# Two half blocks first, casts by DMA, and a GpSimd queue that carries the loads: a fused matmul, gelu, matmul on one core

## The chip, the cores and the metric

The kernel runs on one core of one Trainium2 chip. The metric is the device time of one execution in microseconds (us); the median of several runs is compared. One profiled execution gives the trace. TensorE is the matmul engine, VectorE and ScalarE do element-wise work, GpSimd does some of it too and issues DMAs of its own, and SyncE only issues DMAs.

## The reference

```python
# x: [16, 512, 768] f32, w1: [768, 3072], b1: [3072], w2: [3072, 768]
y = np.matmul(x, w1) + b1
y = 0.5 * y * (1.0 + erf(y / np.sqrt(2.0)))     # gelu
return np.matmul(y, w2).astype(np.float32)
```

The 16 x 512 leading entries are one axis of 8192 rows.

## The kernel before

All matmuls take fp16 operands and add in fp32. To spare TensorE work, both large matmuls use a Strassen-like scheme: 20 products of operand sums take the place of 24 plain products. `P1_WOPS` and `P1_XOPS` list the sums of W1 tiles and of x tiles, `P1_ORD` the 20 products in their order, and `P1_OPS` how partial results in PSUM are copied (C), added (A) and finished (F). `P2_...` are the same for the second matmul.

**First matmul and gelu.** Rows 0 to 511 are done without the scheme, in *plain units*: `plain_unit(u)` for u = 0 to 5, four output tiles each, 6 matmuls of 128x512 per tile (L608). The other rows go in *blocks* of three row groups. `BLK` has six: a half block (256 rows per group), four full blocks (512 rows per group), and a half block. A block has six units (three pairs in a half block). A unit has 60 matmuls of 512 columns (a pair of half units 120 of 256 columns, L739). Each full unit or pair also takes 12 additions with a PSUM operand on VectorE (L318 and L316, into `vt`), 4 copies out of PSUM (L323, ScalarE mostly) and 12 gelu tiles of 512 columns (L444, ScalarE; two instructions of 256 in a half block). `finish` writes gelu to one of `NGST` = 8 buffers, and a store on SyncE's queue (L449, `gd<-ar`) takes it to DRAM. A buffer is free again when its store has landed.

**W1.** `w1_load` brings 24 f32 pieces through SyncE (L374), VectorE or ScalarE casts each (L325, L323), and `w1_ops` makes the 20 operand tiles of each of the six units, 384 columns wide, on VectorE or GpSimd. All six plain units come ahead of the first half block.

**x.** `load_x(b)` casts the rows of a block to fp16 in DRAM by GpSimd DMAs of 256 rows (L593, `xd<-in_x_dram`: 3 for a half block, 6 for a full one) and brings them transposed into SBUF by DMA transposes on SyncE's queue (L595, `ar<-xd`). `x_sums(b)` then makes 13 operand sums per block, on VectorE (one instruction) or GpSimd (three).

**W2.** `w2_build(j)`, eight times, loads a piece of W2 by a GpSimd DMA, makes 12 sums and 2 negated copies on GpSimd, and stores 16 tiles to the DRAM buffer `w2d` by 16 SyncE DMAs (L718).

**Second matmul.** 16 units of 512 rows, 160 matmuls of 128x384 each (L841), 2560 in all. It reads W2's 16 tiles from `w2d` (L785) into the room of W1, and gelu from `gd` (L806), makes 16 sums per unit on VectorE (128x1024), and stores to `out` (L864). The loads are issued by SyncE.

**Order.** All instructions are written out by a planner (`Sched`) when the kernel is built. It keeps a modelled time for each engine and for DMA, and starts the task that can begin first; urgent and background tasks differ by a due time. Its costs (`dve_tt`, `act_ps`, `pool_tt`, the DMA rates) thus decide only the order on each engine. On the chip each engine runs its list in order and waits for the data of each instruction. `add(..., after=, order=)` sets constraints for the planner; only the data that instructions share becomes a wait on the chip.

Of the kernel before, what the change touches and what calls it, by code (L numbers as in the profile page):

```python
# [13 lines left out]
P = 128  # L14
# [9 lines left out]
P1_ORD = [(0, 0, 0), (3, 1, 1), (1, 2, 2), (2, 3, 3), (4, 4, 4), (3, 5, 5), (2, 6, 6), (4, 7, 7), (3, 8, 8), (1, 9, 9), (5, 10, 10), (4, 11, 11), (1, 12, 12), (3, 13, 13), (2, 14, 14), (4, 15, 15), (3, 16, 12), (2, 17, 16), (1, 18, 17), (4, 19, 14)]  # L24
# [5 lines left out]
P1_OPS = [('C', [(1, 0, 2, 0)], -1), ('C', [(1, 0, 3, 0)], -1), ('C', [(1, 0, 3, 2)], -1), ('C', [(1, 0, 4, 0)], -1), ('A', [(-1, 1, 1, 0), (1, 0, 3, 1)], -1), ('A', [(1, 1, 4, 0), (-1, 0, 3, 4)], -1), ('F', [(1, 1, 5, 0)], 0), ('F', [(-1, 0, 2, 3)], 1), ('A', [(-1, 1, 1, 0), (1, 0, 2, 2)], -1), ('F', [(1, 1, 8, 0)], 2), ('A', [(-1, 1, 3, 0), (1, 0, 1, 2)], -1), ('F', [(1, 1, 10, 0)], 3), ('F', [(1, 0, 1, 3)], 4), ('A', [(-1, 1, 3, 0), (1, 0, 4, 1)], -1), ('A', [(1, 1, 13, 0), (-1, 0, 4, 4)], -1), ('F', [(1, 1, 14, 0)], 5), ('F', [(-1, 0, 3, 3)], 6), ('A', [(-1, 1, 2, 0), (-1, 0, 4, 2)], -1), ('F', [(1, 1, 17, 0)], 7), ('F', [(1, 0, 4, 3)], 8), ('A', [(1, 1, 3, 0), (-1, 0, 1, 1)], -1), ('A', [(1, 1, 20, 0), (1, 0, 5, 0)], -1), ('F', [(1, 1, 21, 0)], 9), ('A', [(-1, 0, 1, 0), (1, 1, 0, 0)], -1), ('F', [(1, 1, 23, 0)], 10), ('A', [(1, 0, 0, 0), (1, 1, 1, 0)], -1), ('A', [(1, 1, 25, 0), (-1, 0, 2, 1)], -1), ('F', [(1, 1, 26, 0)], 11)]  # L30
# [54 lines left out]
class Task:  # L85
    __slots__ = ("eng", "fn", "nd", "outs", "reads", "alloc", "frees", "due", "key", "end",
                 "deps", "nbytes", "bulk", "lag", "gen", "started")


class Sched:  # L90


    def __init__(self):
        self.t = {e: 0.0 for e in ("PE", "DVE", "ACT", "POOL", "SP")}
        self.pe = []
        self.pp = 0
        self.avail = {e: [] for e in ("DVE", "ACT", "POOL", "SP")}
        self.dma = [0.0, 0.0, 0.0]
        self.key = 0
        self.left = 0  # L100
        self.pe_ideal = 10.0

    def add(self, eng, fn, reads=(), alloc=None, makes=None, after=(), frees=None, due=None, nbytes=0, bulk=0, order=(), lag=LAT):
# [4 lines left out]
        t.lag = lag  # L108
        t.end = None
# [34 lines left out]
    def _start(self, t, e):  # L144
        r = self.t[e]
        for d in t.deps:
            x = d.end + (0.0 if e in d.eng and len(d.eng) == 1 and e != "SP" else t.lag)
            if x > r:
                r = x
# [7 lines left out]
    def run(self, until=None):  # L157
        drift = 0.0
        while self.left:
# [47 lines left out]
            t.started = r  # L207
            if t.nbytes:
                self.t[e] = r + d
                self.dma[t.bulk] = max(self.dma[t.bulk], r + d) + t.nbytes / (320e3, 250e3, 200e3)[t.bulk]  # L210
# [23 lines left out]
def kernel(  # L234
# [27 lines left out]
    NGST = 8  # L262
    O_BLD = O_GST + NGST * 1024
    NBLD = 10
    O_END = O_BLD + 4608 + NBLD * 768
    NV = 8
# [6 lines left out]
    ident = main.tile([P, P], FP16, name="ident")  # L273
    ps = pps.tile([P, 8, 512], FP32, name="ps")
    gd = [drp.tile([P, HC, 512], FP16, name=f"gd{i}") for i in range(NU)]
    xd = drp.tile([R, K], FP16, name="xd")
    w2d = drp.tile([len(P2_WOUT), P, 8 * NB], FP16, name="w2d")
# [25 lines left out]
    def dve_ps(n):  # L303
        return (n / 0.96 + 215) / 1000

    def act_ps(n):
        return (n / 1.2 + 190) / 1000

    def pool_tt(n):
        return (n * 2.2 + 60) / 1000  # L310
# [24 lines left out]
    def w1_ap(u, w):  # L335
        return a16(O_W1 + (u * 20 + w) * W1T, 384)

    w1op = {}
    w1v = [[Val() for _ in range(20)] for _ in range(6)]
# [5 lines left out]
    WRING = Pool([O_XB + 3072 * i for i in range(6)])  # L345
    SRING = Pool([O_XA + 9216] + [O_SUM + (7 + 2 * i) * 3072 for i in range(4)])
    SRING.put(-1.0, O_BLD + 6144)
# [16 lines left out]
    wch = {}  # L364
    w1cast = []
    w1first = []

    def w1_load(u):
        sv = Val(SRING)
        parts = [Val() for _ in range(4)]  # L370
        for q in range(4):
            f = Val(WRING)
            c0 = (q * 6 + u) * P
            w1first.append(S.add({"SP": 0.45}, lambda e, f=f, c0=c0: nc.sync.dma_start(  # L374
                out=a32(f.slot, 768).rearrange("p (k c) -> p k c", c=P),
                in_=w1.rearrange("(kc p) c -> p kc c", p=P)[:, :, c0:c0 + P]),
                alloc=f, nbytes=P * 768 * 4))
            w1cast.append(S.add({"DVE": 0.50, "ACT": 0.75}, lambda e, f=f, q=q, sv=sv: scale_copy(
                e, a16(sv.slot + q * 1536, 768), a32(f.slot, 768), 1),
                reads=[f], alloc=sv if q == 0 else None, makes=[sv, parts[q]],  # L380
                after=[sv.prods[0]] if q else ()))
        wch[u] = (sv, parts)

    def w1_ops(u, due, after):
        sv, parts = wch[u]
        val = {}
        res = w1op[u] = []
        for i in range(8):
            val[i] = (parts[i // 2], lambda i=i, sv=sv: a16(sv.slot + i * 768, 384))
        outs = {}  # L390
        for w, (i, sg) in enumerate(P1_WOUT):
            outs.setdefault((i, sg), w)
        done = set()
        for (d, op, a, b) in P1_WOPS:
            w = outs.get((d, 1))
            assert w is not None
            va, fa = val[a]
            vb, fb = val[b]
            v = w1v[u][w]
# [503 lines left out]
```

## Time and profile before

| | us |
|---|---|
| median of 8 runs | 963.05 |
| lowest and highest | 961.81, 965.29 |
| profiled execution | 963.69 |
| its span, first to last instruction | 961.9 |
| TensorE busy | 873.5 (91%) |
| VectorE busy | 652.8 (68%) |
| ScalarE busy | 424.8 (44%) |
| GpSimd busy | 255.1 (27%) |

In lines of the profile, PE is TensorE, PEld its weight load, DVE VectorE, ACT ScalarE, POOL GpSimd, and SPq SyncE's DMA issues. L739 is line 739 of the kernel. "out<-in" names the tile or tensor written and read: `ar` is the large SBUF buffer, `ps` PSUM, `vt` partial results, `xd`, `w2d` and `gd` DRAM buffers. In the timeline a row gives start, duration, engine, line and operation, and in brackets how long the engine was idle before and what ended that.

### The profile page before, as it was taken

To read this page: it belongs to the slowest core of one execution; us is meant where nothing else is said; L and a number is where in the kernel's file an instruction comes from. 1 tells how busy PE (TensorE), PEld (TensorE's weight loads), DVE (VectorE), ACT (ScalarE), POOL (GpSimd) and SP (SyncE) were. 2 spreads that over 40 slices of the span, in tenths; PEclk is the share of its full clock that TensorE was granted. 3 is DMA by queue.
4 is the path that set the end of the run, shared out by engine and by line. 5 is a ranking of instruction groups with operands and counts; after the bars stand their busy time and mean duration, and the time that the engine had idled before them with its cause. 6 is when DMAs were issued, how large, how long until landed. Compare 5 with 4: busy or idle time off the path is not lost.

```text
span 961.9 us, 14602 instructions
## 1 busy us (share of the span) xinstructions
PE 873.5 (91%) x4924; PEld 484.9 (50%) x4924; DVE 652.8 (68%) x1009; ACT 424.8 (44%) x773; POOL 255.1 (27%) x270
## 2 busy tenths in 40 slices
PE   6688689788969879979998899999999999999997
PEld 2246534333424334434467566666666666666664
DVE  5989476368637746855677369777777777777763
ACT  5457466566746657757777412111111221211211
POOL 5777656158625600830430000000000000000000
PEclk9899799899979999999999999999999999999999
DMA  9989769887998557454669986555555555566611
GB/s 269 280 198 208 177 184 220 211 234 198 225 200 247 158 168 195 151 131 130 172 215 320 388 330 197 184 170 171 187 182 176 167 189 166 186 197 197 197 66 67
DMA packets 180332, 190.14 MB, mean 198 GB/s; under 512 B 57712, under 2 KB 171120, under 8 KB 173680
## 3 DMA queue, kind: packets, MB, share of 16 engines
q1 hardware_dynamic: 172320, 172.67, 58.0%
q0 software_dynamic: 4848, 16.52, 10.0%
q8 instruction: 38, 0.62, 0.3%
q10 hardware_dynamic: 3088, 0.01, 0.2%
q14 instruction: 38, 0.31, 0.1%
HBM read 106.97 MB, written 98.70 MB: 214 GB/s over the span
## 4 chain that ended last, share of the span: by engine, by line
PE 69%; DMA 11%; DVE 11%; issue 3%; ACT 3%; POOL 2%; DVEq 0%; SPq 0%; ACTq 0%; POOLq 0%
PE ps L841 43%; PE ps L739 23%; DMA gd<-ar 8%; DVE ar L318 6%; DVE vt L318 4%; ACT ar L444 3%; PE ps L608 2%; POOL ar L318 2%; DMA ar<-xd 1%; DMA b1t<-in_b_dram 1%; DVE ar L316 1%; DVE ar L325 1%; ACT vt L323 1%; DMA ar<-in_w_dram 1%; DMA w2d<-ar 0%
## 5 line engine op out<-in xcount | busy, mean ns | idle before, releaser
L739 PE MATMUL ps<-ar 128*128 128x512 f16 (+1 forms) x2160 | 412.6, 353 | 63.3 <-ACT vt L323 27.6
L841 PE MATMUL ps<-ar 128*128 128x384 f16 x2560 | 418.0, 327 | 2.7 <-ACT vt L323 2.7
L739 PEld LDWEIGHTS <-ar 128*128 128x128 f16 x2160 | 215.0, 100 | 260.9 <-issue 79.2
L841 PEld LDWEIGHTS <-ar 128*128 128x128 f16 x2560 | 251.0, 98 | 169.4 <-issue 4.8
L318 DVE TENSOR_TENSOR ar<-ar 128x1024 f16<-128x1024 f16 (+3 forms) x350 | 262.0, 766 | 16.4 <-DMA ar<-xd 9.0
L318 POOL TENSOR_TENSOR ar<-ar 128x384 f16<-128x384 f16 (+2 forms) x206 | 208.8, 1043 | 220.8 <-DMA ar<-xd 101.7
L318 DVE TENSOR_TENSOR vt<-vt,ps 128x512 f32<-128x512 f32 (+1 forms) x260 | 167.5, 644 | 128.5 <-PE ps L739 52.6
L323 ACT ACTIVATE vt<-ps 128x512 f32<-128x512 f32 (+1 forms) x232 | 123.4, 543 | 253.8 <-PE ps L841 229.1
L318 DVE TENSOR_TENSOR vt<-ps,vt 128x512 f32<-128x512 f32 (+1 forms) x230 | 147.6, 642 | 119.0 <-ACT vt L323 52.5
L444 ACT ACTIVATE ar<-vt,b1t 128x512 f16<-128x512 f32 (+1 forms) x288 | 176.3, 645 | 115.6 <-DVE vt L318 81.8
L444 ACT ACTIVATE ar<-ps,b1t 128x512 f16<-128x512 f32 (+1 forms) x168 | 98.8, 614 | 46.0 <-DMA gd<-ar 24.9
L323 ACT ACTIVATE ar<-vt 128x384 f32<-128x384 f32 x48 | 25.1, 523 | 108.2 <-DVE vt L318 87.0
L608 PE MATMUL ps<-ar 128*128 128x512 f16 x144 | 38.0, 424 | 11.0 <-DVE ar L325 11.0
L316 DVE SCALAR_TENSOR_TENSOR vt<-vt,ps 128x512 f32<-128x512 f32 (+1 forms) x46 | 29.3, 637 | 4.2 <-PE ps L841 1.5
L608 PEld LDWEIGHTS <-ar 128*128 128x128 f16 x144 | 14.7, 107 | 33.2 <-DVE ar L325 14.8
L318 DVE TENSOR_TENSOR ar<-vt 128x384 f32<-128x384 f32 x48 | 26.8, 557 | 1.6
L327 POOL TENSOR_SCALAR ar<-ar 128x384 f16<-128x384 f16 x20 | 23.9, 1204 | 13.8 <-DVE ar L325 10.7
L325 DVE CAST ar<-ar 128x768 f16<-128x768 f32 (+1 forms) x24 | 17.6, 742 | 9.3 <-DMA ar<-in_x_dram 5.9
L316 DVE SCALAR_TENSOR_TENSOR ar<-vt,ps 128x384 f32<-128x384 f32 x16 | 8.9, 555 | 21.9 <-PE ps L841 21.7
L323 ACT ACTIVATE ar<-ar 128x384 f16<-128x384 f16 (+2 forms) x31 | 15.9, 556 | 7.5 <-DVE ar L325 3.7
L593 POOL DMA_DIRECT2D xd<-in_x_dram x27 | 13.4, 503 | 0.0
L422 PE MATMUL ps<-ident,ar 128*128 128x128 f16 x60 | 5.9, 255 | 6.5 <-DVE ar L325 5.3
(17 smaller groups left out, 43.5 us busy)
## 6 DMA issues: line engine op xcount, KB each, us to landing
gd<-ar SPq DMA_DIRECT2D x384, 128.0 KB, 2.2
ar<-gd SPq DMA_DIRECT2D x48, 1024.0 KB, 5.6
out_dram<-ar SPq DMA_DIRECT2D x128, 192.0 KB, 5.6
w2d<-ar SPq DMA_DIRECT2D x128, 96.0 KB, 1.8
ar<-w2d SPq DMA_DIRECT2D x16, 768.0 KB, 7.5
xd<-in_x_dram POOLq DMA_DIRECT2D x27, 384.0 KB, 8.5
ar<-in_w_dram SPq DMA_DIRECT2D x24, 384.0 KB, 5.8
ar<-in_w_dram POOLq DMA_DIRECT2D x8, 576.0 KB, 8.6
```

The source lines that it names most:

```text
L316: eng.scalar_tensor_tensor(out=o, in0=a, scalar=-1.0, in1=b, op0=ALU.mult, op1=ALU.subtract)
L318: eng.tensor_tensor(out=o, in0=a, in1=b, op=ALU.add if op == "+" else ALU.subtract)
L323: nc.scalar.activation(out=o, in_=a, func=ACTF.Copy, scale=float(sg))
L325: eng.tensor_copy(out=o, in_=a)
L327: eng.tensor_scalar(out=o, in0=a, scalar1=-1.0, scalar2=None, op0=ALU.mult)
L422: nc.tensor.transpose(out=o[:, kc * P:(kc + 1) * P], in_=nat_ap(kc), identity=ident[:])
L444: ft.append(S.add({"ACT": act_ps(n)}, lambda e, y=y: nc.scalar.activation(out=a16(O_GST + g.slot * 1024 + y * n * 2, n), in_=src[1]()[:, y ...
L593: S.add({"POOL": 1.0}, lambda e, a=a, z=z: nc.gpsimd.dma_start(out=xd[a:z, :], in_=xf[a:z, :]), alloc=c, nbytes=256 * K * 4, bulk=1, after ...
L608: nc.tensor.matmul(out=ps[:, bv.slot, :], lhsT=a16(sv.slot + q * 1536 + kc * 256, P), rhs=a16(O_XT0 + kc * 1024, 512), start=(kc == 0), st ...
L739: nc.tensor.matmul(out=ps[:, bk, y * n:(y + 1) * n], lhsT=w1_ap(u + y, w)[:, kt * P:(kt + 1) * P], rhs=xa[:, kt * n:(kt + 1) * n], start=( ...
L841: nc.tensor.matmul(out=ps[:, bk, 0:NB], lhsT=xa[:, j, :], rhs=a16(w2v[w][1] + j * NB * 2, NB), start=(first and j == 0), stop=(j == 7), sk ...
```

## The change

**Order of the first part.** Plain units and the first half block alternate: plain units 0 and 1, the first pair of the half block, plain units 2 and 3, the second pair, and so on. The last half block moves to second place; the four full blocks follow.

**W1.** The staging now holds pairs of units. Only the first pair comes as f32 through SyncE and is cast by an engine (8 pieces). The other two come by 8 GpSimd DMAs that cast to fp16 on the way. `w1_ops` works on 768 columns, on VectorE alone (plain copies also on ScalarE).

**x.** `x_cast` issues the casts. Those of the second half block stand right behind W1's second pair in GpSimd's queue, those of the first full block right behind W1's third pair. For later blocks the first cast waits for the first x sum of the block two before, by a one-element GpSimd copy that reads that sum (`gated`). The transposes are planned behind given gelu stores of the block before (`mark`). All x sums are on VectorE.

**W2.** The 16 stores of a piece become two GpSimd DMAs (12 tiles made, 6 raw tiles). W2's 16 tiles and the gelu of the first two units of the second matmul are loaded by GpSimd; ten of the tiles and the first unit's loads are paced by one-element reads of gelu buffers of the last block.

**Room and planner.** `NGST` goes from 8 to 7, `NV` from 8 to 7. The planner gets other cost figures and treats the access of VectorE sums and GpSimd operations to SBUF as exclusive (`lock`). The order of units in the second matmul differs: 12, 13 and 14 are last.

GpSimd's list changes from 206 sums, 22 copies and 36 DMAs to 96 sums, 16 negated copies, 17 one-element copies and 84 DMAs. TensorE's instruction count stays.

```diff
-    NGST = 8
+    NGST = 7
-    NV = 8
+    NV = 7
...
+    def gated(gate, fn):
+        for v, ap in gate:
+            o = scr if ap.dtype == FP32 else scr16
+            nc.gpsimd.tensor_copy(out=o[0:1, 0:1], in_=ap[0:1, 0:1])
+        fn()
...
+    def w1_load(p):
...
+                else:
+                    hold = w1first[-1:] if p == 2 or q else x1l[-1:]
+                    w1first.append(S.add({"POOL": 0.85}, lambda e, c0=c0, o=o: nc.gpsimd.dma_start(
+                        out=a16(o, 1536).rearrange("p (k c) -> p k c", c=2 * P), in_=w1r[:, :, c0:c0 + 2 * P]),
+                        makes=[sv, wparts[2 * p][q], wparts[2 * p + 1][q]], nbytes=P * 1536 * 4,
+                        order=hold + sv.prods[:1], **first))
...
-    BLK = [((512, 768, 1024), 256)] + [((r, r + 512, r + 1024), 512) for r in range(1536, 7680, 1536)]
-    BLK.append(((1280, 7680, 7936), 256))
+    BLK = [((512, 768, 1024), 256), ((1280, 7680, 7936), 256)]
+    BLK += [((r, r + 512, r + 1024), 512) for r in range(1536, 7680, 1536)]
...
+    def x_cast(b):
...
+            gate = [blk_sum[b - 2]] if b > 2 and k == 0 else []
+            castq.append(S.add({"POOL": 1.0}, lambda e, a=a, z=z, gate=gate: gated(
+                [(g, a16(g.slot, 768)) for g in gate],
+                lambda: nc.gpsimd.dma_start(out=xd[a:z, :], in_=xf[a:z, :])),
+                alloc=c, reads=gate, nbytes=256 * K * 4, bulk=b > 2, order=w1first[-1:] + castq[-1:],
+                after=castq[-1:] if b > 2 else []))
...
+    w1_load(1)
+    x_cast(1)
+    w1_load(2)
+    x_cast(2)
...
+            m0, dm = {1: (22, 4), 2: (2, 3)}.get(b, (8, 5))
+            mark = blk_stores[b - 1][m0 + dm * k:m0 + dm * k + 1]
...
-            prev = [S.add({"DVE": dve_tt(3 * n), "POOL": 3 * pool_tt(n)}, fn, reads=[va, vb], alloc=v,
-                          order=prev, due=due)]
+            prev = [S.add({"DVE": dve_tt(3 * n)}, lambda e, fa=fa, fb=fb, v=v, op=op: comb(
+                e, a16(v.slot, 3 * n), op, fa(), fb()), reads=[va, vb], alloc=v, order=prev, due=due, lock=True)]
...
-            S.add({"SP": 0.45}, lambda e, fa=fa, w=w: nc.sync.dma_start(
-                out=w2d[w, :, j * NB:(j + 1) * NB], in_=fa()), reads=[va], makes=[w2sv[w]], nbytes=P * 768, bulk=1, lag=4.0)
+        S.add({"POOL": 1.0}, lambda e: nc.gpsimd.dma_start(
+            out=w2d[0:NOUT, :, j * NB:(j + 1) * NB].rearrange("w p n -> p w n"),
+            in_=a16(O_BO, NOUT * 384).rearrange("p (w n) -> p w n", n=NB)),
+            reads=made, frees=[ov], makes=[w2sv], nbytes=P * 768 * NOUT, bulk=1, lag=1.0, due=due)
...
             if b == 0:
-                for y in range(npair):
-                    w1_ops(u + y, S.pe_ideal - 1.0, {4: tr_nat, 5: x0cast}.get(u + y, ()))
+                plain_unit(u)
+                plain_unit(u + 1)
+                if u == 0:
+                    x1_transposes()
+                    xo = x_sums(b, S.pe_ideal, dur)
+                w1_ops(u // 2, S.pe_ideal - 1.0, ([], w1cast, tr_nat + x0cast)[u // 2])
...
-        S.add({"SP": 0.45}, lambda e, w=w, off=off: nc.sync.dma_start(out=a16(off, 8 * NB), in_=w2d[w]),
-              reads=[w2sv[w]], makes=[v], after=after, nbytes=P * W2T)
+        gate = [blk_g[len(BLK) - 1][(25 if w < 5 else 24) + 4 * w]] if w < 10 else []
+        w2l.append(S.add({"POOL": 1.0}, lambda e, w=w, off=off, gate=gate: gated(
+            [(g, a16(O_GST + g.slot * 1024, 512)) for g in gate],
+            lambda: nc.gpsimd.dma_start(out=a16(off, 8 * NB), in_=w2d[dslot[w]])),
+            reads=[w2sv] + gate, makes=[v], after=after, order=w2l[-1:], nbytes=P * W2T))
```

## The prediction

> **What bounds the kernel now.** I read four views in this order: the chain that ended last, the busy time by stage, the timeline of one stall, and the DMA queues. The chain comes first because it says which engine's time is on the path at all.
>
> ```profile
> PE 69%; DMA 11%; DVE 11%; issue 3%; ACT 3%; POOL 2%; DVEq 0%; SPq 0%; ACTq 0%; POOLq 0%
> PE ps L841 43%; PE ps L739 23%; DMA gd<-ar 8%; DVE ar L318 6%; DVE vt L318 4%; ACT ar L444 3%; PE ps L608 2%; POOL ar L318 2%; DMA ar<-xd 1%; DMA b1t<-in_b_dram 1%; DVE ar L316 1%; DVE ar L325 1%; ACT vt L323 1%; DMA ar<-in_w_dram 1%; DMA w2d<-ar 0%
> ```
>
> TensorE carries 69% of the path. The largest foreign piece is `gd<-ar`, the store of gelu results to DRAM. To place the losses I cut the span where the work changes: plain units, first half block, four full blocks, last half block, second matmul.
>
> ```profile
> 0.00:61.00 61.00, 43.04 (x204) 19.05 (x205) 47.13 (x75) 33.89 (x56) 41.58 (x49) 0.94 0.99 259
> 61.00:122.00 61.00, 44.30 (x349) 35.61 (x349) 45.01 (x60) 34.74 (x82) 42.53 (x41) 0.89 0.87 194
> 122.00:204.00 82.00, 68.18 (x291) 29.46 (x290) 45.30 (x66) 46.66 (x79) 40.52 (x47) 0.92 0.87 211
> 204.00:297.00 93.00, 80.75 (x357) 35.32 (x355) 58.81 (x83) 59.27 (x96) 55.48 (x57) 0.94 0.85 215
> 297.00:391.00 94.00, 84.59 (x381) 37.09 (x380) 61.73 (x87) 62.55 (x101) 27.96 (x27) 0.98 0.68 185
> 391.00:487.00 96.00, 89.96 (x408) 40.12 (x407) 63.47 (x90) 66.59 (x108) 42.94 (x48) 0.98 0.48 137
> 487.00:541.70 54.70, 47.46 (x399) 38.91 (x398) 37.85 (x59) 41.94 (x96) 4.06 (x6) 1.00 0.90 314
> 541.70:961.90 420.20, 415.24 (x2544) 249.36 (x2543) 293.49 (x496) 79.16 (x159) 0.00 (x0) 1.00 0.57 184
> ```
>
> Columns: length, then busy time of TensorE, its weight loads, VectorE, ScalarE and GpSimd, the granted clock, DMA share, GB/s. The second matmul is dense: 415 of 420 us. The first 541.7 us are not, and the clock falls to 0.89 to 0.94 where TensorE stops and starts. The timeline shows a typical stop:
>
> ```profile
> 157.69 2.96 POOL L593 DMA_DIRECT2D xd<-in_x_dram  x6
> 161.71 13.35 SPq L449 DMA_DIRECT2D gd<-ar  x6
> 170.53 0.72 ACT L444 ACTIVATE ar<-vt,b1t 128x512 f16<-128x512 f32 x1 [3.71 <-DMA gd<-ar]
> 173.79 0.69 ACT L444 ACTIVATE ar<-ps,b1t 128x512 f16<-128x512 f32 x1 [2.54 <-DMA gd<-ar]
> 174.53 19.72 PE L739 MATMUL ps<-ar 128*128 128x512 f16 x78 [6.02 <-ACT ar L444]
> ```
>
> Six casts of x are issued in 3 us. Then six gelu stores take 13.35 us, the eight gelu buffers fill, gelu waits for a landed store, and TensorE waits for the PSUM bank that gelu should have freed. The same follows the casts at 256, 330 and 417 us. The queues price it:
>
> ```profile
> q0 software_dynamic: 4848, 16.52, 10.0%
> xd<-in_x_dram POOLq DMA_DIRECT2D x27, 384.0 KB, 8.5
> ```
>
> The GpSimd queue (q0) wrote 16.52 MB in 10.0% of 961.9 us on all 16 engines: 96.2 us, 172 GB/s. A cast (0.393 MB) is 2.3 us of every DMA engine, six are 13.7 us.
>
> **Part 1, start and first half block (122 us now).** All engines' work for it, at unhindered rows. TensorE: the first 36 plain matmuls took 10.72 us; the other 108 at 5.34 us for 24 make 24.0; 36 transposes at 0.83 for 12 make 2.5; 360 half-width matmuls at 5.40 for 48 make 40.5. That is 77.7, from 10.96: 88.7. VectorE after the change: 39 W1 sums and 26 x sums, now 768 wide. A lone 384-wide one takes 0.35 us and a 1024-wide 0.687, between them 0.55: 35.9 us. Six negated sums (0.55 at 384; estimate 0.95 at 768) 5.7; 36 PSUM sums at 0.687 24.7; casts and evictions 9: together 75 from 4.3, so 80. ScalarE: 24 gelus at 0.675, 72 half ones at 0.455, 12 PSUM copies at 0.592, 14 W1 casts and copies at 0.84, the rest 9: 77 from 1.2, so 78. No engine alone needs more than 89.
>
> Before loses 33 us against 88.7. Of these 16.3 are TensorE waiting for VectorE's casts (11.0 and 5.3 in the waits). They go: 16 of 24 W1 casts are done by the GpSimd queue's transfers, and plain units alternate with Strassen-like units, so W1 is wanted in three portions. Another 10.2 (`ar<-xd` in the chain) was SyncE standing in transposes behind casts, with gelu stores queued behind it; the transposes now have fixed places later among the stores. In its place comes a new cost: 20 transfers of 0.393 MB (3 of x, 8 of W1, 9 casts) queue on GpSimd from about 18 us: 7.86 MB at 172 GB/s, 45.8 us of all engines. In the stall above a store passed each 2.2 us, or 0.45 per us; from 18 to 64 us that is 21 stores and 7 buffers, against some 33 gelus due: 5 late, 11 us. With a few us of W1 chains I keep about 15 of the 33: **104 us**, bounds 94 and 120.
>
> **Part 2, the second half block right behind.** 360 matmuls 40.5 us; ScalarE 72 at 0.455 and 9 copies 38. It was last and took 54.7, because W2 and gelu loads ran into its stores (9.2 and 9.4 us of `gd<-ar` in the chain there). Its x comes by three casts that are third in the GpSimd queue: 3.9 MB, 23 us alone, 50 when stores share, so by 68; needed near 104. **44 us**, bounds 41 and 50.
>
> **Part 3, four full blocks (365 us now).** Dense stretches (440 to 480 us) hold 94 matmuls in 20.00 us: 0.2128 each, 360 make 76.6, four 306.4; so 59 us are stall and slow clock. VectorE takes over all x sums: per block 72 at 0.685 and 13 at 0.95 (uncontended 1536-wide row) 61.7; ScalarE 24 at 0.592, 48 at 0.718, 24 at 0.67: 64.8. Both stay under 76.6; if VectorE lost that cover, each 1 us more per sum would cost 13 per block. GpSimd keeps 14 operations per W2 piece, about 15 us, eight times. When both run, a 1536-wide sum took 1.29 instead of 0.95, 4 us more per block, hidden too.
>
> Casts are now single between W2 operations, 2.3 us each. Seven buffers at 76.6/72 = 1.06 us a gelu are 7.4; less the median landing of 2.2 and a gelu, 4.5 us of grace remain, so a single cast hides. Not so the W2 staging: its 16 SyncE stores per piece become two on GpSimd, 1.77 MB, 10.3 us at q0's rate. If no gelu store passed meanwhile, 5.8 us would stall per piece, 46 in all; with 0.45 per us passing, the grace stretches to 8.6 us and 1.7 stalls, 14 in all; if the plain copy runs faster than the casts, nothing. I take 14 and 2 for block borders: **322 us**, bounds 306 and 352. Waits added: 17 single-element GpSimd copies that read a W1 tile, an x sum or a gelu buffer. Behind the first are the 20 early transfers (its wait is in the 18 us), behind three more casts and W2 operations that are wanted a block later, behind the last thirteen only loads for the second matmul, placed late by intent; if those hold too long, part 4's upper bound pays. I take nothing.
>
> *Rule against it.* The issue times of the 27 casts are 486, 486 and 592 ns (minimum, median, maximum), though VectorE was mostly busy. The Trainium skill, "SBUF — State Buffer", section "SBUF: two separate sides", says that a VectorE operation in a two-port mode locks GpSimd out of writing the descriptors of its own DMAs. By it, 48 more GpSimd transfers wait, and with 0.95 us each (an estimate) the first twenty would put 19 us on part 1. The row shows no such stretch, so the sum has zero.
>
> **Part 4, second matmul.** Same 2560 matmuls, 16 units in another order; 420.2 us. W2 and first gelu loads go to GpSimd, paced by the last block's gelus, so its start wait of 2.7 us stays or goes; the second unit's three loads come after all W2 loads: 6 tiles and 3 loads, 7.9 MB, 25 us at the 314 GB/s of the window before, against 26 us for the first unit. Bounds 419 and 424; I keep **420.2**.
>
> Sum 104 + 44 + 322 + 420.2 = 890.2. The profiled execution took 963.69 for its span of 961.9, 1.8 outside; it lies 0.6 above the median of 963.05. Forecast **892**.
>
> **Rivals.** *The start stays bound by DMA and by VectorE's chain.* DMA share was already 0.99 and 0.87 there. Part 1 at 120, block two at 48, full blocks at 335: 925. For it: the 45.8 us queue. Against: less is asked of VectorE. Chance 0.28, range 912 to 945.
>
> *The GpSimd queue starves gelu stores (slower).* Place: first 470 us. Its traffic there grows to 38 pieces of 0.393 MB, 4.72 of W2 in and 14.16 out: 33.8 MB, 197 us at 172 GB/s against 96. Before, `gd<-ar` outside the last block held 62.2 us of the chain (80.8 less 18.6): 0.65 per us of that queue. At the same rate 128 us fall on a stall-free 88.7 + 40.5 + 306.4 + 420.2 = 855.8: 986 with the outside. It decides from (961.9 - 855.8)/197 = 0.54. Against: the rate comes from bunches of six. Chance 0.06.
>
> *It doesn't do what it says*: the plan's order lets waits fall where buffers free, and loss only moves; 963. Chance 0.01.
>
> **Numbers.** Forecast case 0.65, its own range 870 to 912. The range 868 to 932 takes it in and half of the first rival. A difference under 0.2% is about what a measurement of this kernel can't tell from none. Faster 0.93, same 0.01, slower 0.06.
>
> **What would show it.** Right: block one ends near 104 us and two near 148; no gelu wait on `gd<-ar` over 5 us after 150; TensorE windows of 19 to 20 in 20 us there; second matmul starts near 470. Wrong: `gd<-ar` still above 5% of the chain; waits under W2 stores; VectorE sums ending TensorE's waits; a second matmul longer than 424.

## The result, and the profile after

The changed kernel takes 973.95 us (median of 11 runs, 967.06 to 979.42) against 962.72 for the kernel before (32 runs beside it): ratio 1.0116, 95% interval 1.0093 to 1.0140. It is slower by 1.2%, where 892 us was forecast. Executions over 1.5% slower than the fastest of their kernel, two single ones of over 3 ms among them, are left out of all ratios: one of twelve here, five of ten in casts_eighth, two of ten in w2_stores_eighth (the profiles of these two kernels are of such executions), at most one of any other changed kernel. The profiled execution of the changed kernel took 970.23 us, with a span of 968.4. All ratios below are to the kernel before; 0.001 is 0.96 us.

The span cut where TensorE's timeline changes stage: start with first half block, second half block, four full blocks, second matmul. The columns are those of the table of stages before.

```profile
0.00:110.00 110.00, 84.19 (x561) 56.12 (x562) 68.15 (x124) 68.06 (x127) 23.99 (x39) 0.91 1.00 207
110.00:167.00 57.00, 43.68 (x371) 36.72 (x370) 30.61 (x42) 35.94 (x86) 23.23 (x29) 0.94 0.98 207
167.00:272.00 105.00, 82.74 (x351) 35.41 (x351) 64.38 (x89) 58.38 (x95) 46.84 (x54) 0.91 0.92 212
272.00:367.00 95.00, 83.55 (x361) 36.32 (x361) 63.51 (x83) 59.89 (x97) 58.12 (x62) 0.95 0.81 209
367.00:450.00 83.00, 78.60 (x361) 34.99 (x360) 63.75 (x91) 59.76 (x97) 4.68 (x4) 1.00 0.53 157
450.00:545.00 95.00, 84.89 (x379) 37.59 (x378) 61.16 (x91) 62.45 (x102) 14.34 (x35) 0.96 0.76 259
545.00:968.40 423.40, 416.59 (x2544) 249.63 (x2543) 295.01 (x499) 79.46 (x160) 0.00 (x0) 0.99 0.52 175
```

The parts are 110, 57, 378 and 423 us where 104, 44, 322 and 420 were forecast. The third full block is the control: GpSimd is nearly idle in it (4.68 us, 4 instructions), the clock is 1.00, and it takes 83. In its neighbours, where GpSimd works and transfers, the same block takes 95 to 105. So the loss stands where GpSimd works, not where there is more matmul; whether it comes from there is for the experiments.

The DMA queues, then the waits (engine, line, what it waited for: us, times, longest):

```profile
q1 hardware_dynamic: 138176, 134.91, 46.6%
q0 software_dynamic: 17648, 52.70, 22.9%
```
```profile
ACT ar L481 <- DMA gd<-ar: 71.6, 40, 9.2
POOL ar L775 <- DMA w2d<-ar: 30.6, 3, 12.0
PE ps L833 <- DVE ar L329: 16.6, 12, 3.6
```

The first of these rows in the kernel before:

```profile
ACT ar L444 <- DMA gd<-ar: 51.5, 19, 8.9
```

GpSimd's queue (q0) has grown from 16.52 to 52.70 MB, and from 10.0% to 22.9% of the engines' time. ScalarE's gelus wait 71.6 us in 40 waits for a gelu store to land; before it was 51.5 us in 19.

The shares of the chain that ended last, by engine and by line, need care:

```profile
PE 55%; DMA 4%; DVE 3%; ACT 1%; issue 1%; ACTq 0%; DVEq 0%
PE ps L950 43%; PE ps L833 12%; DMA gd<-ar 4%; DVE vt L329 2%; DVE ar L329 1%; ACT ar L481 1%; ACT vt L334 0%; DVE vt L327 0%; ACTq L481 0%; DVEq L329 0%; DVEq L327 0%; ACTq L334 0%
```

The shares sum to 64%: followed backwards, this chain breaks off at 338 us. Its 4% of `gd<-ar` is no sum over the stages in which the loss is, and can't be set beside the 8% of before. The timeline of a stall can:

```profile
199.10 1.60 SPq L661 DMA_TRANSPOSE ar<-xd  x1
199.53 0.57 POOL L624 DMA_DIRECT2D xd<-in_x_dram  x1
200.09 1.09 POOL L797 DMA_DIRECT2D w2d<-ar  x1
200.79 4.13 SPq L486 DMA_DIRECT2D gd<-ar  x5
201.18 0.84 POOL L801 DMA_DIRECT2D w2d<-ar  x1
205.02 7.71 SPq L661 DMA_TRANSPOSE ar<-xd  x1
211.22 0.69 ACT L481 ACTIVATE ar<-ps,b1t 128x512 f16<-128x512 f32 x1 [8.45 <-DMA gd<-ar]
213.97 0.76 POOL L775 DMA_DIRECT2D ar<-in_w_dram  x1 [11.95 <-DMA w2d<-ar]
215.24 3.14 PE L833 MATMUL ps<-ar 128*128 128x512 f16 x7 [8.84 <-ACT vt L334]
```

GpSimd issues a cast and both stores of a W2 piece within 2.5 us: here the cast is not single. On SyncE's queue one x transpose then needs 7.71 us to issue (median of all 27: 1.44, longest 8.24), gelu is idle 8.45 us, and TensorE 8.84. The stores issued from 199 to 216 us land after a median of 8.6 us; over the whole run it is 2.8, and 1.7 in the third full block:

```profile
gd<-ar SPq DMA_DIRECT2D x10, 128.0 KB, 8.6
```

From 202.75 to 205.5 us no DMA engine starts a packet at all. The packet records of the trace show 24 packets of the transpose and one of the cast under way through this gap; what holds the other engines, they don't show. A similar picture stands at 118 to 130 us.

### The profile page after: what moved, and what is told of

It reads as the page before. It is cut to its first block, busy times and chain, and to the rows that moved or that the text cites. A ratio compares the mean times of both kernels' runs of the same rounds, so it can differ in the third digit from the quotient of the medians.

```text
span 968.4 us, 14183 instructions
## 1 busy us (share of the span) xinstructions
PE 874.2 (90%) x4924; PEld 486.8 (50%) x4924; DVE 646.6 (67%) x1016; ACT 424.0 (44%) x758; POOL 171.2 (18%) x219
## 3 DMA queue, kind: packets, MB, share of 16 engines
q1 hardware_dynamic: 138176, 134.91, 46.6%
q0 software_dynamic: 17648, 52.70, 22.9%
q10 hardware_dynamic: 3088, 0.01, 0.2%
## 4 chain that ended last, share of the span: by engine, by line
PE 55%; DMA 4%; DVE 3%; ACT 1%; issue 1%; ACTq 0%; DVEq 0%
PE ps L950 43%; PE ps L833 12%; DMA gd<-ar 4%; DVE vt L329 2%; DVE ar L329 1%; ACT ar L481 1%; ACT vt L334 0%; DVE vt L327 0%; ACTq L481 0%; DVEq L329 0%; DVEq L327 0%; ACTq L334 0%
## 5 line engine op out<-in xcount | busy, mean ns | idle before, releaser
L329 DVE TENSOR_TENSOR ar<-ar 128x1024 f16<-128x1024 f16 (+2 forms) x373 | 263.1, 728 | 8.2 <-ACT ar L334 1.9
L329 POOL TENSOR_TENSOR ar<-ar 128x384 f16<-128x384 f16 x96 | 88.1, 947 | 60.7 <-DMA ar<-in_w_dram 59.9
L357 POOL COPY scr<-ar 1x1 f16<-1x1 f16 (+1 forms) x17 | 5.7, 337 | 240.1 <-ACT ar L481 143.2
L674 PE MATMUL ps<-ar 128*128 128x512 f16 x144 | 33.7, 395 | 1.5 <-ACT ar L334 1.5
L338 POOL TENSOR_SCALAR ar<-ar 128x384 f16<-128x384 f16 x16 | 21.4, 1348 | 0.0
L334 ACT ACTIVATE ar<-ar 128x768 f16<-128x768 f16 (+2 forms) x18 | 13.7, 767 | 5.4 <-DMA ar<-in_x_dram 3.5
```

The lines of the kernel that those rows point to most:

```text
L329: eng.tensor_tensor(out=o, in0=a, in1=b, op=ALU.add if op == "+" else ALU.subtract)
L334: nc.scalar.activation(out=o, in_=a, func=ACTF.Copy, scale=float(sg))
L338: eng.tensor_scalar(out=o, in0=a, scalar1=-1.0, scalar2=None, op0=ALU.mult)
L357: nc.gpsimd.tensor_copy(out=o[0:1, 0:1], in_=ap[0:1, 0:1])
L674: nc.tensor.matmul(out=ps[:, bv.slot, :], lhsT=a16(O_WS[u // 2] + q * 3072 + kc * 512 + u % 2 * 256, P), rhs=a16(O_XT0 + kc * 1024, 512), ...
```

## The experiments

**Which of GpSimd's transfers cost.** In four kernels one group of transfers is made small or moved. In w2_stores_eighth the W2 loads read the first piece eight times, in casts_eighth all transposes read the first cast. The four share one theory (GpSimd's transfers starve the gelu stores) and its rivals: VectorE's sums or the block order.

```diff
# w2_stores_eighth: 14 of 16 W2 stores move 48 of 384 columns
-            out=w2d[0:NOUT, :, j * NB:(j + 1) * NB].rearrange("w p n -> p w n"),
-            in_=a16(O_BO, NOUT * 384).rearrange("p (w n) -> p w n", n=NB)),
+            out=(w2x[j, 0:NOUT] if j else w2d[0:NOUT, :, 0:NB]).rearrange("w p n -> p w n"),
+            in_=a16(O_BO, NOUT * 384).rearrange("p (w n) -> p w n", n=NB)[:, :, 0:48 if j else NB]),
...
# casts_eighth: 26 of 27 casts
-                lambda: nc.gpsimd.dma_start(out=xd[a:z, :], in_=xf[a:z, :])),
+                lambda: nc.gpsimd.dma_start(out=xd[a:z, :], in_=xf[a:z, :]) if a == 1280 else
+                nc.gpsimd.dma_start(out=xj[a // 8:z // 8, :], in_=xf[a:a + 32, :])),
...
# last_loads_eighth: ten W2 tile loads, and the first unit's gelu loads likewise
-            lambda: nc.gpsimd.dma_start(out=a16(off, 8 * NB), in_=w2d[dslot[w]])),
+            lambda: nc.gpsimd.dma_start(out=a16(off, 8 * NB if w >= 10 else NB),
+                                        in_=w2d[dslot[w]][:, 0:8 * NB if w >= 10 else NB])),
...
# w2_stores_sync: both stores of a piece on SyncE's queue, same bytes
-        S.add({"POOL": 1.0}, lambda e: nc.gpsimd.dma_start(
+        S.add({"SP": 0.45}, lambda e: nc.sync.dma_start(
```

> The changed kernel, but of the 16 GpSimd stores of W2 sums only the two of the first piece are whole; the other fourteen write an eighth of their bytes to a buffer nobody reads, and W2's loads repeat the first piece. The list of every other engine is unchanged. Theory A (long GpSimd-queue transfers keep gelu stores from landing, gelu stops, TensorE stops): the waits of gelu on a store between 110 and 360 us (about 40 us in the changed kernel's trace) fall by half or more, and TensorE is done with the first matmul 15 to 30 us earlier; time about 950. Theory B (the first matmul is held by VectorE, which now makes all x sums; store waits only stand in front of that): under 6 us earlier, time above 966. W2's loads get smaller pieces here, so the last block may be slower; the stage is judged at the end of the fourth-last unit row, before those loads.

> The changed kernel, but only the first cast of x is whole; 26 casts move an eighth of their bytes to a buffer nobody reads, and every transpose reads the rows of the first cast. No list of another engine changes. Theory A: the early stop of gelu at 57 to 67 us (9.2 us) goes, the half block behind it falls from 57 us towards 44, and later blocks gain 2 us a cast where a W2 transfer stood beside it: 20 to 30 us in all, time about 948. Theory B: the transposes no longer wait for casts, so x sums come earlier and VectorE is relieved at block borders, 10 us or more, but gelu's waits on stores stay above 50 us. Neither: under 5 us.

> The changed kernel, but the loads that GpSimd issues during the last block (three of gelu for the first unit of the second matmul, the first ten W2 tiles) move an eighth of their bytes. Lists and waits are unchanged. Theory A: the four stops of gelu at 477 to 544 us (6.7, 6.8, 5.9 + 6.7, 9.9 us in the chain) go with the exception of the last, which stands beside the six loads that stay whole; the last block falls from 83 us to about 62 to 65 over its dense 77, that is 15 to 22 us less, time about 955. Theory B: the same last block within 5 us.

> The changed kernel with the 16 stores of W2 sums issued by SyncE instead of GpSimd, same bytes and shapes; the planner places them anew. Theory A1 (it is GpSimd's own DMA ring, served in turn with SyncE's, that holds the gelu stores up): 8 to 20 us faster, about 958. Theory A2 (it is the bytes, whichever queue carries them): no better, as gelu stores then stand behind them in SyncE's own queue; within 6 us of 974 or slower. Theory B: within 4 us of 974.

| kernel | ratio (95%) | against the change, us |
|---|---|---|
| w2_stores_eighth | 0.9927 (0.9899 to 0.9955) | -18 |
| casts_eighth | 0.9830 (0.9788 to 0.9872) | -28 |
| last_loads_eighth | 1.0048 (1.0009 to 1.0088) | -7 |
| w2_stores_sync | 1.0013 (0.9990 to 1.0036) | -10 |

One figure in the expectation of last_loads_eighth was a slip: a last block of 62 to 65 us lies below its 77 us of dense matmul; 15 to 22 us less was meant. From last gelu to last gelu the block fell from 92.5 to 85.7 us, but in this pair of profiles the first full block grew from 105.9 to 113.2. The casts, priced at nothing in the full blocks by the forecast, cost some 28 us. That figure rests on five executions of 939.0 to 951.6 us; with the other four, of 953.8 to 960.7, the median is 951.6 and the saving 22. So it isn't shown that the casts cost more than the W2 stores. Of the 18 us of the W2 stores, 10 come back when they stand in SyncE's queue and not in GpSimd's; the bytes are the same.

**All at once, the block order, and the buffer.**

```diff
# half_last: the second half block last again
-    BLK = [((512, 768, 1024), 256), ((1280, 7680, 7936), 256)]
-    BLK += [((r, r + 512, r + 1024), 512) for r in range(1536, 7680, 1536)]
+    BLK = [((512, 768, 1024), 256)] + [((r, r + 512, r + 1024), 512) for r in range(1536, 7680, 1536)]
+    BLK.append(((1280, 7680, 7936), 256))
...
# gst6
-    NGST = 7
+    NGST = 6
# all_eighth: small casts, W2 stores and first gelu loads; all_eighth_half_last: with half_last
```

> Left out: 26 of the 27 casts of x and 14 of the 16 W2 stores move an eighth of their bytes to tensors that nothing reads, all x transposes read the one whole cast, and the first unit's gelu loads move an eighth; the instructions stay in their order, and the arithmetic on the engines is unchanged. Theory A (the transfers of GpSimd's queue starve the gelu stores and x transposes of SyncE's queue): the three savings seen one by one (casts 0.029 of the time before, W2 stores 0.019, last loads 0.007) add up, ratio about 0.957, some 921 us; ACT's gelus wait for gelu stores less than 20 us in all against 71.6; no x transpose is issued for over 5 us. If the three stalls stand in for one another, the sum is not reached: 0.965 to 0.98. Theory B (the order of the blocks costs the time: six transposes and 13 x sums of a full block squeezed into the 45 us of the short block, VectorE full): the first full block still takes over 98 us, and the whole is not under 0.96.

> The changed kernel with the second half block put back to the last place; the casts behind the W1 loads, the gating by x sums, the whole-queue W2 staging and the seven gelu buffers all stay, and the planner orders the rest again. Theory A (GpSimd's transfers): the same transfers stand in the same queue, so the time stays within 8 us of the changed kernel (ratio 1.00 to 1.02), and the gelu wait for stores stays over 60 us. Theory B (the block order): the first full block no longer has its sums and transposes squeezed in, so the span falls by 12 to 25 us, ratio 0.985 to 1.00, with the first full block under 97 us after a 112 us start.

> One gelu buffer fewer again, 6 for 7. Theory A with a thin cushion (the buffers are what the starved stores run out of): each buffer is worth 0.6 us of grace in each of some 20 to 25 stalls, so 8 to 15 us slower than the changed kernel, ratio 1.02 to 1.03, and ACT's gelus wait over 85 us for stores against 71.6. If buffers do not matter: within 3 us of the changed kernel, ratio 1.009 to 1.015.

> all_eighth and half_last in one: an eighth of the bytes in GpSimd's queue as there, and the second half block last. Theory A alone: within 5 us of all_eighth. Theory B beside A: 12 to 25 us under all_eighth, near 900 us, which would be the forecast's 892 within its reach. If the block order is worth something the other way (the short block early is good once the queue is empty): 5 to 15 us above all_eighth.

all_eighth: 0.9622 (0.9594 to 0.9650), 926.4 us. The single savings nearly add up: 48 us of 52. Gelu's waits for stores fall from 71.6 to 24.2 us (under 20 was expected), and the longest issue of a transpose from 8.24 to 5.25. half_last, in which the gates, the room for x sums and the order of units in the second matmul follow the block order: 1.0105 (1.0064 to 1.0147), the same as the change; with small transfers it is some 7 us worse than all_eighth (0.9691, 0.9650 to 0.9733). So the order of the blocks is no cause, and the theory that it was falls. gst6: 1.0257 (1.0217 to 1.0297), gelu's waits for stores 82.8 us: one buffer fewer costs 14 us, so the kernel lives off this cushion.

**What starves a store: bytes, packets, or transposes ahead of it?** The queue rows of the kernels differ in the W2 stores alone, which gives the size of a packet. On ACT's queue (w2_stores_act, queue q10):

```profile
q1 hardware_dynamic: 138176, 134.91, 46.3%
q0 software_dynamic: 14320, 38.54, 18.2%
q10 hardware_dynamic: 21776, 14.17, 4.9%
```

GpSimd's queue loses 3328 packets for 14.16 MB: 4.25 KB each on average, at (22.9% of 968.4 less 18.2% of 954.3) x 16 / 3328 = 0.23 us of an engine. On ACT's the same stores are 18688 packets (21776 less 3088 in the changed kernel's q10 row), 758 bytes each. A packet of q1 takes 46.6% x 968.4 x 16 / 138176 = 0.052 us. A full block's gelu store is 8 packets on each of 16 engines, 0.42 us alone. With one W2 packet of q0 after each of its own it takes 8 x 0.28 = 2.3 us by this estimate; a new gelu comes each 1.06 us. The stall above shows it, from 208.25 to 213 us, where W2's stores and gelu stores run together:

```profile
DMA packets 721, 1.94 MB, mean 408 GB/s; under 512 B 49, under 2 KB 372, under 8 KB 721
```

Packets of 512 B to 2 KB are those of the gelu stores, 323; larger ones are those of W2's stores, 349. That is about one for one, and 323 packets are 2.5 stores in 4.75 us, 1.9 us each.

Casts are coarser still. In the stall of the kernel before, from 159.5 to 172 us, only casts stand in q0:

```profile
DMA packets 394, 2.37 MB, mean 190 GB/s; under 512 B 96, under 2 KB 306, under 8 KB 306
q0 software_dynamic: 167, 2.14, 83.8%
```

Of the 88 packets over 8 KB, 87 are q0's, some 24.6 KB each (16 to a cast) and 83.8% x 12.5 x 16 / 87 = 1.9 us of an engine. Beside them only 210 packets of gelu stores start, 2.4 for each of a cast: 1.6 stores in 12.5 us, one each 7.6 us. So the prediction's 2.2 us per store (13.35 / 6) is the pace at which SyncE issued the stores, not the pace at which they moved. In casts_eighth q0 has the same 17648 packets as in the change and only those of the casts are shorter; so in q0 it is the length of a packet that costs.

The Trainium skill, "DMA: Bandwidth & Descriptors", section "Queues, rings and completion order", says that each engine serves the queues that have work in turn, a whole packet at a time; the row of W2's stores agrees, the row of the casts has more than one packet of a store to each of a cast. Two kernels test the turns from the side of the stores, with the same bytes in each; a third moves the stores to ACT's queue:

```diff
# gelu_stores_eighth: 128 partitions, an eighth of each row
-            out=gd[un][:, t:t + k, c0:c0 + n],
+            out=gx[un][:, t:t + k, c0 // 8:(c0 + n) // 8] if un else gd[un][:, t:t + k, c0:c0 + n],
...
# gelu_stores_16p: 16 partitions, whole rows
-            out=gd[un][:, t:t + k, c0:c0 + n],
-            in_=a16(O_GST + g.slot * 1024, 512).rearrange("p (t r) -> p t r", r=n)),
+            out=gx[un][:, t:t + k, c0:c0 + n] if un else gd[un][:, t:t + k, c0:c0 + n],
+            in_=a16(O_GST + g.slot * 1024, 512).rearrange("p (t r) -> p t r", r=n)[0:16 if un else P]),
...
# gelu_stores_act: the whole stores, issued on ACT
-        stores.append(S.add({"SP": 0.45}, lambda e: nc.sync.dma_start(
+        stores.append(S.add({"ACT": 0.1}, lambda e: nc.scalar.dma_start(
```

> Left out: the gelu stores of all units but the first move an eighth of their bytes to tensors that nothing reads, and the second matmul reads the first unit's gelus for every unit; every instruction stays on its queue in its order, and all of GpSimd's transfers stay whole. Theory A (what the 4.5 us of gelu buffers cannot cover is a slow gelu store, whoever slows it): with short stores the ACT waits on them fall from 71.6 to under 20 us and the whole comes to 900 to 925 us, ratio 0.935 to 0.96, though GpSimd's queue is as full as before. Rival T (the stores wait in SyncE's order behind x transposes that GpSimd's transfers delay, up to 8.2 us of issue): the transposes' long issues stay, and so do over 40 us of the waits; ratio over 0.985.

> Left out: as in the kernel whose gelu stores move an eighth, the stores of all units but the first go to tensors that nothing reads and the second matmul reads the first unit's gelus; but here a store moves 16 of 128 partitions in whole 1 KB pieces (an eighth of the packets) instead of 128 partitions in 128-byte pieces (all the packets, an eighth of the size), which came to 0.9919. Theory Q in its packet form (each of the 16 engines takes a turn of SyncE's queue, one packet, and a turn of GpSimd's, some 4 KB and 0.2 us; a store of 8 packets per engine then takes 1.6 us and more whatever the packets' size): one packet per engine, no starving; ratio 0.945 to 0.965, ACT's gelus wait under 25 us for stores. Theory bytes: as the other eighth, 0.985 to 0.998. Rival T (x transposes held up in SyncE's order hold up the stores behind them): waits over 40 us stay, 0.985 or more.

> All gelu stores issued from ACT's queue, whole; transposes stay on SyncE's. Nothing left out. Theory T: the stores no longer stand behind transposes of up to 8.2 us of issue; the waits on stores fall by half, ratio 0.985 to 1.000, unless ACT's own issue (0.4 us each in the kernel whose W2 stores were on ACT, 384 of them, 154 us) makes ACT the bound of the full blocks, which would be 1.03 or more. Theory Q: one row of turns against GpSimd's as before; within 0.6% of the changed kernel plus what ACT pays, 1.01 to 1.03.

An eighth of the size: 0.9919 (0.9883 to 0.9954). An eighth of the packets: 0.9685 (0.9627 to 0.9743). SyncE's queue and the waits of ScalarE, first for the small packets, then for the few:

```profile
q1 hardware_dynamic: 138176, 93.63, 36.4%
ACT ar L481 <- DMA gx<-ar: 50.5, 24, 7.9
```
```profile
q1 hardware_dynamic: 89792, 93.63, 35.3%
ACT ar L481 <- DMA gx<-ar: 34.8, 22, 7.4
```

Both store kernels move 93.63 MB on q1 and leave q0 whole, yet fewer packets bring back 41 us and smaller ones 19. So of a store the number of packets counts for more than the bytes. The expectation of gelu_stores_eighth (900 to 925 us) missed for this reason. That of gelu_stores_16p missed by a little too: 0.945 to 0.965 was expected of the turns, and waits under 25 us. Of the 34.8 us that stay, a part may be the rival of transposes in SyncE's order, since issues of 10.08 and 7.95 us still stand there; as the whole cause it is out, for it expected 0.985 or more and waits over 40 us. How large its part is stays open: a kernel without the transposes was not tried. gelu_stores_act was to separate it and did not: 1.1762 (1.1667 to 1.1857). ACT now waits for its own gelu before stores (80.5 us in 153 waits), and its gelus wait another 64.1 us, in 7 waits, for x transposes.

**Other queues and other times for the same transfers.**

```diff
# w2_stores_act: both stores of a piece on ACT's queue
-        S.add({"POOL": 1.0}, lambda e: nc.gpsimd.dma_start(
+        S.add({"ACT": 0.3}, lambda e: nc.scalar.dma_start(
# casts_paced
-            gate = [blk_sum[b - 2]] if b > 2 and k == 0 else []
+            gate = [blk_g[b - 2][(len(blk_g[b - 2]) // 6) * k + 3]] if b > 2 else []
...
# last_loads_sync: W2 tile loads, and the first two units' gelu loads likewise
-        gate = [blk_g[len(BLK) - 1][(25 if w < 5 else 24) + 4 * w]] if w < 10 else []
-            lambda: nc.gpsimd.dma_start(out=a16(off, 8 * NB), in_=w2d[dslot[w]])),
+        gate = []
+            lambda: nc.sync.dma_start(out=a16(off, 8 * NB), in_=w2d[dslot[w]])),
```

> The two W2 stores of each piece issued from ACT's queue in place of GpSimd's; the same bytes, and nothing left out. On SyncE's queue they gave 1.0013 against 1.0116 on GpSimd's, with an eighth of the bytes 0.9927. Theory Q (the share between queues decides: a GpSimd packet holds some 4 KB against 1 KB of a gelu store, and a piece's store on SyncE stands ahead of the gelu stores): on a queue of their own with 768-byte pieces they delay gelu stores least, ratio 0.990 to 1.000. Theory bytes (what moves at the same time costs the same from any queue): like SyncE's, 1.000 to 1.006. If ACT pays for issuing 16 more DMAs with about 1 us each, 1.01 or more.

> The 18 casts of blocks three to five each wait for a gelu output, every 12th (in the short block every 6th) of the block two before, in place of one wait for an x sum and then cast behind cast. Theory A with a cushion (single bursts of 8.5 us each hide in part in the gelu buffers, rows of them do not): 8 to 15 us of the 27 that all casts' bytes are worth come back, ratio 0.995 to 1.003. Theory A without a cushion (each cast costs its stall wherever it stands): within 4 us of the changed kernel, 1.008 to 1.016. If GpSimd's wait for gelu outputs holds buffers and W2 pieces back: slower than 1.016.

> The W2 tile loads and the first two units' gelu loads issued from SyncE's queue without gates, as the kernel before does, in place of GpSimd's queue gated by gelu outputs. With an eighth of the bytes of 13 of them the gain was 0.007. Theory Q (GpSimd's large packets starve the gelu stores): half to all of that comes back, ratio 1.004 to 1.009. Theory order (a 768 KB load in SyncE's queue holds the gelu stores behind it by 3 us or more each): 1.012 to 1.025, the last block over 88.9 us.

w2_stores_act: 0.9960 (0.9938 to 0.9981), 15 us better than the change and already faster than the kernel before. The Trainium skill, same page, section "Issuing engines are not separate DMA queues", says that another issuing engine only saves the time of issuing. These runs disagree: GpSimd, SyncE and ACT give 1.0116, 1.0013 and 0.9960 with the same two stores per piece. Issuing them takes GpSimd some 1 us each, but the time doesn't follow that: w2_stores_eighth leaves the issues on GpSimd and is 18 us faster than the change. casts_paced is slower: 1.0258 (1.0219 to 1.0298), the last of the three cases expected, with gelu's waits for stores at 102.4 us in all. GpSimd's own waits for gelus grow from 143.2 to 229.2 us, as that case assumed. So spreading the casts brought nothing back; how much of the 14 us lost is the casts' own toll and how much GpSimd's waits stays open. last_loads_sync: 1.0117 (1.0079 to 1.0156), no difference from the change; both expected mechanisms may be at work and cancel, which was not separated.

**More buffers.**

```diff
# gst8_inplace; gst8_w2_act adds the ACT queue
-    NGST = 7
-    BLD = 15360
+    NGST = 8
+    BLD = 14592      # 7 kept in the place of -7, negated last
...
# gst9_w2_act
+    NGST = 9
+    BLD = 13824      # 6 kept in the place of -0, copied last; identity in free staging
...
```

> Eight gelu buffers as in the kernel before, seven in the changed one; room for it comes from one temporary of the W2 staging kept in the place of an output that is written from it last, and one x-sum slot fewer late in the run. The order of instructions is nearly that of the changed kernel. Six buffers came to 1.0257, seven to 1.0116: theory C (the cushion is what the starved stores run out of, each buffer worth the same) gives 0.996 to 1.004 and ACT's waits on stores near 60 us. If the worth falls with each: 1.004 to 1.010.

> Eight gelu buffers and the W2 stores on ACT's queue together, nothing left out. If the two add: 0.996 less 0.008 to 0.016, so 0.980 to 0.990, faster than both kernels. If they cure the same stalls: 0.990 to 0.996.

> As the kernel with eight gelu buffers and the W2 stores on ACT's queue, with a ninth buffer; its room comes from the other temporary of the W2 staging, kept where a copy is written last, and from the identity matrix, kept in the staging space that is free until the transposes on TensorE are done. Nothing left out. Six, seven and eight buffers came to 1.0257, 1.0116 and 0.9946, eight with the stores on ACT to 0.9828. If a ninth is worth as much as the eighth: 0.966 to 0.974. If the worth falls off: 0.974 to 0.981. If the planner's order, the same as with eight on VectorE and ACT, leaves nothing to use it: 0.981 to 0.985.

gst8_inplace: 0.9946 (0.9915 to 0.9977), gelu's waits for stores 60.2 us; gst8_w2_act: 0.9828 (0.9769 to 0.9888); gst9_w2_act: 0.9755 (0.9731 to 0.9779), 939.03 us, 24 us faster than the kernel before and 35 than the change. In gst9_w2_act gelu waits a third as much:

```profile
ACT ar L481 <- DMA gd<-ar: 25.5, 16, 9.4
```

The steps from six to eight buffers are worth 14 and 16 us; with W2 on ACT's queue the eighth is worth 13, and the ninth 7, which is about the uncertainty of that step. The room for the eighth and ninth was found by small changes elsewhere (one x-sum slot fewer late in the run, among others), so a step is not the buffer alone. With that reserve, the change's own step from eight to seven cost some 16 us, and its W2 stores on GpSimd cost 15 against ACT's queue, 10 against SyncE's; with eight buffers and ACT's queue the rest of the change is a gain of 17 us.

**Is that all?** all_eighth_16p makes both sides small: GpSimd's transfers as in all_eighth, the stores as in gelu_stores_16p.

> Left out: as in the kernel with an eighth of the bytes in GpSimd's casts, W2 stores and first gelu loads (0.9622), and the gelu stores of all units but the first move 16 of 128 partitions as well (alone 0.9685). What is left is the forecast's own sum without starved stores: start 104, second half block 44, four full blocks of 76.6 to 78, second matmul 420 to 424 and 2 outside, 892. If starving was all that failed: 885 to 905 us, ratio 0.92 to 0.94. If another 20 us and more is lost elsewhere (x transposes, VectorE's sums in the first full block, W2 loads): 912 to 922 us, ratio over 0.948.

0.9468 (0.9442 to 0.9494), 911.9 us, between the two expected ranges. Its stages:

```profile
0.00:108.00 108.00, 91.09 (x642) 63.50 (x643) 74.35 (x134) 74.03 (x141) 32.79 (x49) 0.95 0.73 146
108.00:155.00 47.00, 37.05 (x301) 29.86 (x300) 30.79 (x39) 32.33 (x77) 20.37 (x23) 0.96 0.62 118
155.00:487.00 332.00, 318.50 (x1440) 141.61 (x1439) 243.19 (x344) 235.10 (x380) 129.92 (x149) 0.98 0.39 84
487.00:910.70 423.70, 415.42 (x2544) 249.29 (x2543) 296.25 (x502) 80.91 (x162) 0.00 (x0) 0.99 0.54 178
```

So of the 82 us that the forecast missed, 62 (1.0116 less 0.9468) come back when GpSimd's transfers and the gelu stores are both small, and 20 are in the sum itself.

## Why the prediction was wrong

**Part 1 (104, came 110, bounds 94 to 120).** Held. TensorE's waits for VectorE's casts went from 16.3 us to 5.0. The early queue was priced at 11 us late. In all_eighth the stage ends 11 us sooner by its last gelu (101.1 for 112.5). In the change the six casts of the first full block are issued at 39 to 51 us, and gelu is idle 9.21 us until 67.

**Part 2 (44, came 57, bounds 41 to 50).** Failed. The step counted only the block's own three casts. In fact the first W2 piece's stores, a cast and an 8.24 us transpose fall into it; with small transfers and stores it takes 47.

**Part 3 (322, came 378, bounds 306 to 352).** The step that decided. Five of its terms:
- *"so a single cast hides"*: zero was taken. Small casts saved 22 to 28 us over the whole run. The 4.5 us of grace assumed stores that land in 2.2 us and were counted afresh for each cast; but some casts come back to back with W2's stores, and in the stall at 199 to 216 us the median landing was 8.6. Nor did spreading the casts bring anything back (casts_paced).
- *The rate, "0.45 per us"* of stores that pass beside q0. It was read from the issues of the stall before. The packets of 1.6 stores moved there in 12.5 us, 0.13 per us. Beside W2's stores it was 2.5 in 4.75 us, 0.53 per us; so for the W2 staging the figure fitted by luck, and for casts it was more than three times too high. Part 1 rests on it as well.
- *The buffers.* The grace was computed with seven, but the step from eight to seven was given no price: 16 us.
- *TensorE at 0.2128 us per matmul.* That was a stretch at full clock. Even in all_eighth_16p the full blocks ran at 318.5 / 1440 = 0.2212, clock 0.98: 12 us. The clock is not all of it: the third block of the change had 1.00 and took 78.60 / 361 = 0.2177. In the change the busy rows of all four blocks give 329.8 / 1452 = 0.2271, with clocks of 0.91, 0.95, 1.00 and 0.96 in blocks of 105, 95, 83 and 95 us; so some of the loss is a slower clock where the stalls are.
- *VectorE's cover.* All x sums on VectorE were called hidden. In all_eighth_16p TensorE waited 11.6 us for sums in three of the four full blocks, at their starts; in the change 14.8 us from 170 to 545.

The W2 staging, put at 14 with a bound of 46, was sized about right: 18 for its stores alone. The failed step is thus that GpSimd's transfers were priced each by its own grace, the casts at nothing, where the runs show them holding up the gelu stores: 48 us with the transfers small, 62 with the stores small too. How much of it goes by way of x transposes that stand before the stores in SyncE's queue stays open. The prices overlap and must not be added.

**Part 4 (420.2, came 423.4, bounds 419 to 424).** Held.

**The rule against it.** Zero for GpSimd being locked out of writing descriptors was right as far as the row goes: the 27 casts took 523 ns each to issue, within the 486 to 592 of before.

**The rivals.** "The GpSimd queue starves gelu stores" was the right mechanism, with a price (986) 12 us above what came, and had a chance of 0.06. The price is partly luck: it takes casts and W2's stores to cost the same per us of q0, but beside casts a store passes each 7.6 us and beside W2's stores each 1.9. The argument against it, that its rate comes from bunches of six, was the mistake: 1.9 us per store against 1.06 us per gelu, beside two transfers of one W2 piece, is no matter of bunches. The first rival named 120, 48 and 335 and was wrong on place: VectorE did not bound the start.

**Signs.** Block one near 104 and two near 148, no gelu wait over 5 us after 150, second matmul from near 470: all came out wrong (110, 167, 8.45, 545). Of the signs of being wrong, VectorE's sums ended waits of TensorE (16.6 us), and waits stood under W2 stores. "`gd<-ar` above 5% of the chain" did not show, but the chain broke off at 338 us; the table of waits showed it.

## What to carry to other kernels

Before moving DMAs to another queue, look at who shares the engines with them and in which packets. Here a small, urgent stream of 1 KB packets beside q0's packets of 4.6 KB got about a fifth of the engines' time, and beside packets of 24.6 KB a twentieth (5.5% in the stall before), however few bytes it had. Read the pace of such a stream from packets or landings, not from issues. Price a buffer of such a stream by the stalls it covers, not by its room; here one buffer was worth some 16 us, about what the rest of the change gained. And a "hidden" transfer has to be checked against the rate of the stream beside it, not against a grace that is counted anew for each.

## What the runs showed of the hardware

- The same W2 stores are packets of 4.25 KB on average on GpSimd's queue and of 758 bytes on SyncE's and ACT's; the kernels came to 1.0116, 1.0013 and 0.9960.
- A cast of 256 rows in DRAM on GpSimd's queue is one packet of 24.6 KB on each engine, 1.9 us long in the stall before; from 159.5 to 172 us there, 1.6 gelu stores moved.
- Cutting the bytes of the gelu stores by eight at the same number of packets was worth 19 us, cutting their packets by eight at whole size 41.
- An x transpose on SyncE took up to 8.24 us to issue in the change where GpSimd's transfers ran, and 1.39 to 1.72 us in the block in which GpSimd was idle.
- Of the 16 W2 stores issued from ACT in w2_stores_act, each took 0.37 to 0.47 us to issue, with no wait shown before it. With all 384 gelu stores on ACT, ACT waited 80.5 us for its own gelus before them, in a kernel at 1.1762.
